# The recurrent stage of a two-block network: TensorE's order written by hand as bursts between groups of eight large matmuls

## The chip, the core and the metric

The kernel runs on one core of a Trainium2 chip. The metric is device time in microseconds (us) of one launch. A core has five engines with instruction queues of their own: TensorE (PE; its weight loads are shown apart as PEld), VectorE (DVE), ScalarE (ACT), GpSimd (POOL) and SyncE (SP). Each runs its instructions in the order of its queue. DMA transfers are issued from one of these queues and wait there for what they depend on.

## What is computed

Two transformer blocks on 512 tokens of width 1024, all in fp32. The first block (two layers of attention with a feed-forward part) is not touched by the change. The second is cut here to what matters:

```python
h = rms_norm_2(x, pre_mix_norm)
p_r, p_k, p_v, p_c, z_rwkv, z_conv = split(h @ w_in)       # 1024 each, p_c 2048
y_rwkv = rwkv7_time_mix(h, p_r, p_k, p_v, ...)             # 16 heads of 64; S is 64x64 for each head
  # step t:  S = S*w_t + (S a_t) b_t + v_t k_t ;  y_t = S r_t ; group norm; + bonus; * g ; @ w_rwkv_out
y_conv = conformer_conv(p_c, ...)                          # u*sigmoid(gate), causal conv of 31 taps over the
                                                           # tokens, layer norm, silu, @ w_conv_out
merged = sigmoid(z_rwkv) * y_rwkv + sigmoid(z_conv) * y_conv
x = x + rms_norm_2(merged @ w_out, post_mix_norm)
x = x + rms_norm_2(ffn(rms_norm_2(x)), post_ffn_norm)
```

The first line to the last but one are the stage that this text calls the recurrent stage.

## The kernel before

**Large products.** A 1024x1024 weight is taken in blocks of 1024x128. `wload` loads a block (SP's queue) into one of two `raw` buffers; ScalarE rounds it to the high half `wh` (L160), VectorE subtracts to get the low half `wl` (L161). A product of such a block with the 512 tokens (`hT_h`, `hT_l`: the halves of h) is 24 matmuls of 128x512: high by high (L274), high by low (L275) and low by high (L277), summed in one PSUM bank. `h`, `l` and `raw` have two buffers each.

**The recurrence in chunks.** The 512 tokens are eight chunks of 64; heads go in pairs j = 0..7 and pairs in groups of two, g = 0..3. `pair_in(j)` makes r, k, v and the gates of a pair from large products. `pair_out(j)` makes decays (L979 to L987), bonus (L1006), the 64x128 Gram matmuls (L1024) and transposes to token order (L1040). `solve(g)` inverts the unit triangular 64x64 matrices of a group: their 16x16 diagonal blocks by forward substitution on VectorE, in 15 steps of a product (L1093) and a reduction (L1095), each as two instructions for the two halves of the partitions. The blocks go through DRAM into that layout and back (L1076, L1085, L1097, L1100, on GpSimd's queue). Then two sets of 64 small 32x32 matmuls (L1107, L1113; below: quads) and an identity product ahead of the first (L1104) join 16x16 blocks to 32x32 ones, VectorE transposes (L1102, L1118), and further small matmuls (L1143 among them) join the rest. `chain(g)` runs over the chunks in order: four small matmuls (L1160, L1169), a copy of half the result by ScalarE (L1171) and half by VectorE (L1172), four more (L1176), an addition on VectorE (L1179, with `ds` made by GpSimd, L1165), four outputs (L1182). A chunk needs the one ahead of it. `post(g)` normalises and gates the outputs (L888 ff.).

**The conv branch.** `conv_in(f)` makes c = u * sigmoid(gate) for 128 channels and stores it in DRAM; `conv(f)` loads it into a tile `c` (one buffer, SP's queue) and runs 30 VectorE instructions over 128x512 (L1228, the taps). The sum over channels, mean, and layer norm follow after the last.

**The end of the stage.** 16 gates z (`gate`), `mapped` by w_rwkv_out into `cm`, layer norm, `mapped` by w_conv_out, the sum `m` split into `mer_h`, `mer_l`, and the product with w_out (`rows_proj`, `ready` holding half of its weights).

**What sets the order.** The code calls these functions in an order given by the strings `ORD` and the counts `FI` (conv_in and gates) and `CV` (conv). Every engine's order then comes from a scheduler which goes by readiness and by the offsets `O` that `high_priority` gives to each function. On TensorE it puts small matmuls singly between large ones wherever they become ready. All the stage's DMAs but the weights and a few loads are issued from GpSimd's queue (`DQ`).

Of the kernel before, what the change touches and what calls it, by code (L numbers as in the profile page):

```python
# [72 lines left out]
def _constants():  # L73
    oh, mask = _t5_onehot()
    i = np.arange(P)
    same = i[:, None] // 64 == i[None, :] // 64
    blk = np.concatenate([same, i[:, None] % 32 < 16, i[:, None] % 32 == np.arange(32),
                          (i[:, None] == i[None, :]) - same / 64], 1).astype(np.float32)
    tri = (i[:, None] % 64 < np.arange(65)[None, :]).astype(np.float32)
    return {"c_t5_oh": oh, "c_t5_mask": mask, "c_nb_mask": _nb_masks(), "c_blk": blk, "c_tri": tri}  # L80
# [7 lines left out]
def tile_two_blocks(ctx: ExitStack, tc: tile.TileContext, A, out):  # L88
# [36 lines left out]
    W["n"] = 0  # L125

# [24 lines left out]
    def wload(src, a, b, views=None, into=None):  # L151
# [454 lines left out]
    with ExitStack() as es:  # L606
# [206 lines left out]
        blk = pm.tile([P, 2 * P + 33], F32, name="blk")  # L813
# [49 lines left out]
    with ExitStack() as es:  # L863
        es.enter_context(lows)
# [4 lines left out]
        nc.vector.memset(smask[:, ::C], 0.0)  # L869
        two = blk[:, :P:64]  # L870
        i32 = blk[:, P + 1 : P + 33]
        centre = blk[:, P + 33 :]
        BANKS.update(ps=[0, 1, 2], po=[3, 4, 5], ca=[6], cb=[7], cc=[6, 7])

        def col_rstd(sq, rhs, eps, op, expand, role="po", scale=1.0):

            ps = pst(role)
# [3 lines left out]
            r = cs.tile([P, 8], F32, tag="r8" + role, name="r8")  # L881
# [4 lines left out]
            ps = pst(role)  # L886
# [7 lines left out]
        with ExitStack() as es2:  # L894
            el = es2.enter_context(tc.tile_pool(name="el", bufs=1))

            SH = 1

            def et(tag, n=T, bufs=1):
                return el.tile([P, n], F32, tag=tag, name=tag, bufs=bufs)  # L900

            def shifted(src, scale=None, **kw):

                sh = el.tile([P, T + 2], F32, tag="sh", name="sh", bufs=SH)
                nc.gpsimd.memset(sh[:, 0:1], 0.0)
                nc.scalar.activation(sh[:, 1 : T + 1], src, AF.Copy, **({} if scale is None else {"scale": scale}))
                return sh[:, 0:T]

            def group_tiles(g):
                q = g % 2  # L910
                G = Ctx()
                X_ = big_tile(f"X{q}", [P, 2, NC_, 2, P])
                G.X = lambda i: X_[:, i]
                G.SV, G.BKT = (big_tile(f"{n}{q}", [P, 2, NC_, 2, C]) for n in ("SV", "BKT"))
                ra = big_tile(f"RA{q}", [P, 2, 2, NC_, C])
                G.RB, G.AB = ra[:, 0], ra[:, 1]
                G.D2 = cs.tile([P, 2, NC_], F32, tag=f"D2{q}", name="D2", bufs=1)
                return G

            def chunks(t):  # L920
                return t.rearrange("p (c t) -> p c t", t=C)

            def pair_in(j):

                fs = slice(j * P, (j + 1) * P)

                def one(v):
                    return V_[v][:, j : j + 1]

                rkv = et("rkv", 3 * T + 2 * C, 2)  # L930
                nc.gpsimd.memset(rkv[:, 0:C], 0.0)
                nc.gpsimd.memset(rkv[:, C + 3 * T :], 0.0)
                for i in range(3):
                    dst_ = rkv[:, C + i * T : C + (i + 1) * T]
                    hl = ahead.pop(0) if ahead else wload(wcols(w_in, 0, KD, i * D + j * P, P), KD, P)
                    o = proj_units([hl])[0]
                    sh = shifted(o, scale=one(("mu_r", "mu_k", "mu_v")[i]))
# [475 lines left out]
```

## Time and profile before

| | us |
|---|---|
| median of 3 runs | 2462.03 (2459.45 to 2467.74) |
| profiled execution, own time | 2471.44 |
| its span, first to last instruction | 2469.7 |
| of it: ahead of the recurrent stage (0 to 1272.5) | 1272.5 |
| the recurrent stage (1272.5 to 2047.7) | 775.2 |
| behind it (product with w_out, feed-forward part) | 422.0 |

All numbers of the trace come from the profiled execution. TensorE is busy 96% of the span and VectorE 51%; a mean granted TensorE clock of 0.972 belongs to it. In the rows below, times are us from the start of the span; "busy" of a matmul can overlap the next one's, since they are pipelined, so the distance of two starts tells what one costs.

### The profile page before, as it was taken

To read this page: it belongs to the slowest core of one execution; us is meant where nothing else is said; L and a number is where in the kernel's file an instruction comes from. 1 tells how busy PE (TensorE), PEld (TensorE's weight loads), DVE (VectorE), ACT (ScalarE), POOL (GpSimd) and SP (SyncE) were. 2 spreads that over 40 slices of the span, in tenths; PEclk is the share of its full clock that TensorE was granted. 3 is DMA by queue.
4 is the path that set the end of the run, shared out by engine and by line. 5 is a ranking of instruction groups with operands and counts; after the bars stand their busy time and mean duration, and the time that the engine had idled before them with its cause. 6 is when DMAs were issued, how large, how long until landed. Compare 5 with 4: busy or idle time off the path is not lost. (4 is left out here: it accounts for less than half of the span.)

```text
span 2469.7 us, 34315 instructions
## 1 busy us (share of the span) xinstructions
PE 2377.3 (96%) x13667; PEld 1869.2 (76%) x13667; DVE 1250.3 (51%) x2083; ACT 934.9 (38%) x1681; POOL 287.2 (12%) x455
## 2 busy tenths in 40 slices
PE   7899999999999999999999899999989999999998
PEld 6756888888887788888886676666667777888887
DVE  4376532143434642223446877588587764422232
ACT  4365432142344542222346344444344343422231
POOL 1000120000100000000012223233142101000000
PEclk9999999999999999999999999899799999999999
DMA  7320763143542263332232222123125454533321
GB/s 202 107 77 35 217 185 98 55 134 106 154 120 79 65 184 96 94 102 93 70 91 82 76 90 71 60 72 92 54 80 174 124 171 148 162 96 95 100 95 60
DMA packets 294240, 263.39 MB, mean 107 GB/s; under 512 B 13904, under 2 KB 260756, under 8 KB 293696
## 3 DMA queue, kind: packets, MB, share of 16 engines
q1 hardware_dynamic: 274648, 208.82, 28.3%
q0 software_dynamic: 10352, 30.02, 3.8%
q10 hardware_dynamic: 9080, 22.37, 3.0%
q8 instruction: 107, 1.75, 0.3%
q14 instruction: 53, 0.43, 0.1%
HBM read 226.33 MB, written 34.83 MB: 106 GB/s over the span
## 5 line engine op out<-in xcount | busy, mean ns | idle before, releaser
L274 PE MATMUL p<-hT_h,wh 128*128 128x512 f32 (+1 forms) x1776 | 686.7, 391 | 7.0 <-DVE cc L1218 3.3
L275 PE MATMUL p<-hT_l,wh 128*128 128x512 f32 (+1 forms) x1776 | 685.7, 390 | 0.0
L161 DVE TENSOR_TENSOR wl<-raw,wh 128x1024 fp32r<-128x1024 f32 (+2 forms) x348 | 410.8, 1184 | 424.5 <-ACT wh L160 360.2
L160 ACT ACTIVATE wh<-raw 128x1024 fp32r<-128x1024 f32 (+2 forms) x348 | 352.2, 1015 | 633.9 <-PE p L275 418.9
L277 PE MATMUL p<-hT_h,wl 128*128 128x512 f32 (+1 forms) x1776 | 449.1, 388 | 7.7 <-DVE wl L161 7.7
L274 PEld LDWEIGHTS p<-hT_h,wh 128*128 128x128 f32 x1776 | 340.3, 192 | 75.4 <-DVE cc L1218 4.5
L275 PEld LDWEIGHTS p<-hT_l,wh 128*128 128x128 f32 x1776 | 340.2, 192 | 66.1 <-issue 2.5
L277 PEld LDWEIGHTS p<-hT_h,wl 128*128 128x128 f32 x1776 | 322.4, 190 | 73.2 <-DVE wl L161 8.1
L168 PE MATMUL p<-wh,fh 128*128 128x512 f32 x528 | 206.1, 390 | 1.5 <-ACT memv L376 0.8
L169 PE MATMUL p<-wl,fh 128*128 128x512 f32 x528 | 205.9, 390 | 0.0
L170 PE MATMUL p<-wh,fl 128*128 128x512 f32 x528 | 205.2, 389 | 0.0
L1228 DVE SCALAR_TENSOR_TENSOR acc<-c,dwc,acc 128x512 f32<-128x512 f32 x240 | 186.0, 775 | 4.5
L300 DVE TENSOR_TENSOR fT<-sg,p 128x384 f32<-128x384 f32 (+1 forms) x88 | 46.8, 552 | 258.7 <-PE p L277 249.5
L192 POOL TENSOR_SCALAR rstd<-ss 128x1 f32<-128x1 f32 x24 | 9.2, 383 | 1445.6 <-ACT junk L188 1445.5
L175 DVE TENSOR_TENSOR fl<-fT,fh 128x512 fp32r<-128x512 f32 x66 | 45.1, 691 | 144.4 <-ACT fh L174 144.4
L168 PEld LDWEIGHTS p<-wh,fh 128*128 128x128 f32 x528 | 99.1, 188 | 23.0 <-ACT memv L376 1.2
L169 PEld LDWEIGHTS p<-wl,fh 128*128 128x128 f32 x528 | 99.1, 188 | 20.3
L170 PEld LDWEIGHTS p<-wh,fl 128*128 128x128 f32 x528 | 99.1, 188 | 20.3
L174 ACT ACTIVATE fh<-fT 128x512 fp32r<-128x512 f32 x66 | 40.8, 628 | 182.7 <-PE p L169 174.8
L168 PE MATMUL p<-wh,hT_h 128*128 128x256 f32 (+1 forms) x256 | 91.7, 359 | 2.6 <-ACT v L536 2.0
L169 PE MATMUL p<-wl,hT_h 128*128 128x256 f32 (+1 forms) x256 | 90.2, 353 | 0.6 <-DVE wl L161 0.6
L170 PE MATMUL p<-wh,hT_l 128*128 128x256 f32 (+1 forms) x256 | 89.0, 351 | 0.0
(328 smaller groups left out, 3053.5 us busy)
## 6 DMA issues: line engine op xcount, KB each, us to landing
raw<-in_w_gu SPq DMA_DIRECT2D x88, 512.0 KB
raw<-in_w_in SPq DMA_DIRECT2D x56, 512.0 KB
raw<-in_w_down SPq DMA_DIRECT2D x44, 512.0 KB
raw<-in_ffn_w_gate SPq DMA_DIRECT2D x22, 512.0 KB
raw<-in_ffn_w_up SPq DMA_DIRECT2D x22, 512.0 KB
raw<-in_ffn_w_down SPq DMA_DIRECT2D x22, 512.0 KB
raw<-in_w_in_b SPq DMA_DIRECT2D x20, 512.0 KB
xs<-xt POOLq DMA_DIRECT2D x19, 512.0 KB, 4.0
```

The costliest lines, as they stand in the source:

```text
L160: nc.scalar.activation(to(h), fr(raw), AF.Copy)
L161: nc.vector.tensor_tensor(to(l), fr(raw), to(h).bitcast(F32), ALU.subtract)
L168: nc.tensor.matmul(ps, lhsT=lh, rhs=rh, start=start, stop=False)
L169: nc.tensor.matmul(ps, lhsT=lh, rhs=rl, start=False, stop=False)
L170: nc.tensor.matmul(ps, lhsT=ll, rhs=rh, start=False, stop=stop)
L174: nc.scalar.activation(h, src, AF.Copy)
L175: nc.vector.tensor_tensor(l, src, h.bitcast(F32), ALU.subtract)
L274: nc.tensor.matmul(o[:, c], lhsT=h[:, k, :], rhs=hT_h[:, k, c], start=k == 0, stop=False)
L275: nc.tensor.matmul(o[:, c], lhsT=h[:, k, :], rhs=hT_l[:, k, c], start=False, stop=False)
L277: nc.tensor.matmul(o[:, c], lhsT=l[:, k, :], rhs=hT_h[:, k, c], start=False, stop=k == KD - 1)
L300: nc.vector.tensor_tensor(dst(fT[:, f, :]), src(sg), src(ps[1]), ALU.mult)
L1228: nc.vector.scalar_tensor_tensor(acc, c[:, t : t + T], dwc[:, t, f : f + 1], acc, ALU.mult, ALU.add)
```

## The change

TensorE's order in the recurrent stage is no longer the scheduler's but that of the code (`manual_schedule` for PE alone; the other engines are scheduled as before). `drive()` walks through a list of units (a unit is one product of 24 large matmuls), and every unit yields after each eight. At a yield, the five streams `chains, outs, solves, posts, ends` are asked in turn; each issues a burst of its small matmuls if its own due time has come, by a count of time in which a group of eight takes `QUANTUM` = 1.85 and a burst the first number of its own yield; the second number is how long the stream then rests. A unit's weights are issued one unit ahead. The list is: pairs and conv_ins mixed, 16 gates, eight maps by w_conv_out, eight by w_rwkv_out. Small parts change along with it:

- The subtraction for `wl` goes in turn to VectorE and to GpSimd.
- `solve` substitutes in 8x8 blocks: 7 steps of two VectorE instructions on all partitions. Six quads instead of two (256 small matmuls more in each solve) and a second identity product join them; `at` and `ttd` are moved by four DMAs each instead of two; the transposes of L1118 go, and three PSUM copies that VectorE makes (L1213 in the new code, L1222 twice) come in, besides ScalarE's.
- The three gate weights of a pair come in one tile; `col_rstd` is two bursts (`sums`, `per_token`); `post` loads its two inputs into the group's free `X` tiles; the taps are paced one at a time; `cc` has two buffers.
- The conv branch is mapped first; the merged result goes into `hT_h`, `hT_l`. Layer norm sits in the stream `ends` and begins while the last chain runs.

```diff
+    W["sub"] = [nc.vector]
-            nc.vector.tensor_tensor(to(l), fr(raw), to(h).bitcast(F32), ALU.subtract)
+            W["sub"][W["n"] % len(W["sub"])].tensor_tensor(to(l), fr(raw), to(h).bitcast(F32), ALU.subtract)
...
+        W["sub"] = [nc.vector, nc.gpsimd]
...
+        def dense(hl, xh=..., xl=..., cut=KD):
+            (h, l), ps = hl, pst()
...
+                        n += 2 - part
+                        if n % 8 == 0 and n < 3 * KD:
+                            yield
+            return ps
...
-                for t in range(1, 16):
-                    p3 = pr[:, : t * t].rearrange("p (j s) -> p j s", s=t)
-                    for q in parts:
-                        nc.vector.tensor_tensor(p3[q], tt[q, :t, :t], at[q, None, :t, t].to_broadcast([q.stop - q.start, t, t]), ALU.mult)
-                    for q in parts:
-                        nc.vector.tensor_reduce(tt[q, :t, t], p3[q], AX.X, ALU.add)
+            for t in range(1, 8):
+                p4 = pr[:, : 2 * t * t].rearrange("p (m j s) -> p m j s", m=2, s=t)
+                nc.vector.tensor_tensor(p4, tt[:, :, :t, :t], at[:, :, None, :t, t].to_broadcast([P, 2, t, t]), ALU.mult)
+                nc.vector.tensor_reduce(tt[:, :, :t, t], p4, AX.X, ALU.add)
...
+            nc.vector.transpose(dt, dd)
+            yield 0, SOLVE_LAT
+            de = s2("de")
+            nc.scalar.activation(de, quad(of(e), of(dt), True), AF.Copy)
+            yield 1.3, 2.5
+            pa, pb = quad(of(de), of(dd)), quad(of(dd), of(de))
+            dd, dt = s2("dd"), s2("dt")
+            nc.vector.tensor_copy(dt, pb)
+            nc.scalar.activation(dd, pa, AF.Copy)
+            yield 1.2, 2.5
+            de = s2("de")
+            nc.scalar.activation(de, quad(lambda i: diag[i], of(dt), True), AF.Copy)
+            yield 1.3, 2.5
+            pb, pa = quad(of(dd), of(de)), quad(of(de), of(dd))
...
+                for t in range(1, 31):
+                    nc.vector.scalar_tensor_tensor(acc, c[:, t : t + T], dwc[:, t, f : f + 1], acc, ALU.mult, ALU.add)
+                    yield None, TAP
...
+        CCB, SOLVE_LAT, CHAIN_LAT, TAP = 2, 25.0, 1.8, 1.3
+        QUANTUM, GAP = 1.85, 1
...
+            hl, since, idle = units[0][0](), 0, 0.0
+            for i, (_, run, pre) in enumerate(units):
+                while pre is not None and not pre():
+                    now += 0.5
+                    idle += 0.5
+                    burst()
+                nxt = units[i + 1][0]() if i + 1 < len(units) else None
+                for _ in run(hl):
+                    now += QUANTUM
+                    since += 1
+                    if since >= GAP:
+                        since = 0
+                        burst()
+                hl = nxt
...
+        with tc.manual_schedule(engines={mybir.EngineType.PE}):
+            drive()
```

The names in the rows below are tiles with a running number; `p` is a PSUM bank. TensorE's queue before, in group 0's chain while a pair's product runs (L1176 is a state update, L1182 an output):

```order
L1176 MATMUL p_12447<-SV_11129,BKT_11130 64x64
L274 MATMUL p_13160<-hT_h,wh 128x512
L1176 MATMUL p_12447<-SV_11129,BKT_11130 64x64
L275 MATMUL p_13160<-hT_l,wh 128x512
L1176 MATMUL p_12447<-SV_11129,BKT_11130 64x64
L274 MATMUL p_13160<-hT_h,wh 128x512
L1176 MATMUL p_12447<-SV_11129,BKT_11130 64x64
```

In the order after, a chain's bursts stand as follows (L1278 reads the state, L1282 and L1301 make outputs, L1163 and L1166 are the identity product and a quad of group 1's solve, L934 and L935 large):

```order
L1278 MATMUL p_12104<-SV_9831,X_9830 64x64 x4
L1282 MATMUL p_12105<-X_9830,SV_9831 64x64 x4
L1163 MATMUL p_12120<-blk,ident 128x512
L1166 MATMUL p_12120<-dt,e 32x32 x64
L934 MATMUL p_12095<-hT_h,wh 128x512
L935 MATMUL p_12095<-hT_l,wh 128x512
L934 MATMUL p_12095<-hT_h,wh 128x512
L935 MATMUL p_12095<-hT_l,wh 128x512
L934 MATMUL p_12095<-hT_h,wh 128x512
L935 MATMUL p_12095<-hT_l,wh 128x512
L934 MATMUL p_12095<-hT_h,wh 128x512
L935 MATMUL p_12095<-hT_l,wh 128x512
```

Where single small matmuls stood between single large ones, whole bursts now stand between groups of eight; the burst behind this group (L1295, the state update into p_12104) reads what VectorE copies out of L1278's result.

VectorE's queue before, at a copy of the chain (L1172; L1228 are taps, L1218 ends a conv_in, L1011 and L997 belong to a pair_out):

```order
L1228 SCALAR_TENSOR_TENSOR acc<-c,dwc,acc 128x512 x2
L1218 TENSOR_TENSOR cc<-p_11851,cc 128x512
L1172 COPY SV_9831<-p_11074 64x2x64
L1228 SCALAR_TENSOR_TENSOR acc<-c,dwc,acc 128x512
L1011 TENSOR_TENSOR X_12581<-rkv,le 128x8x64
L1228 SCALAR_TENSOR_TENSOR acc<-c,dwc,acc 128x512 x2
L997 TENSOR_TENSOR ls<-ls,rkv 128x512
```

VectorE's queue after, at the place of the bursts above (L1347 are taps, L1290 the chain's copy, L1298 its addition, L1205 and L1213 belong to the solve):

```order
L1347 SCALAR_TENSOR_TENSOR acc<-c,dwc,acc 128x512 x4
L1290 COPY SV_9831<-p_12104 64x2x64
L1347 SCALAR_TENSOR_TENSOR acc<-c,dwc,acc 128x512 x2
L1205 STREAM_TRANSPOSE dt<-dd 128x512
L1347 SCALAR_TENSOR_TENSOR acc<-c,dwc,acc 128x512 x8
L1298 TENSOR_TENSOR SV_9831<-p_12104,ds 64x2x64 x2
```

Ten taps and a transpose stand between the copy and the addition of one chunk.

GpSimd's queue after, in a solve (L1201 and L1204 move the substituted blocks out and back):

```order
L893 TENSOR_TENSOR r_10663<-r_10663,neg_half 128x8
L1201 DMA ttd_9683<-tt 64x8x8 x4
L163 TENSOR_TENSOR wl<-raw,wh 128x1024
L1204 DMA dd<-ttd_9683 32x16x32 x4
L1107 DMA bvd_9635<-so 128x512
```

Before, the same two DMA steps (L1097, L1100) had one store between them; now a weight's subtraction stands there.

## Rows read from the trace of the kernel before

**Rows 1.** Stretch: us, busy (instructions) of PE, PEld, DVE, ACT, POOL, clock, DMA share, GB/s.

```profile
1272.50:2047.70 775.20, 733.99 (x5543) 528.41 (x5542) 566.30 (x1001) 346.25 (x628) 198.69 (x281) 0.94 0.32 95
```

**Rows 2.** TensorE's waits in the recurrent stage: total us, times, longest.

```profile
PE p L277 <- DVE wl L161: 7.7, 1, 7.7
PE p L888 <- ACT ysq L884: 5.8, 5, 2.2
...
```

**Rows 3.** Timeline of TensorE, large matmuls alone: start, us of one.

```profile
1299.77 0.40 PE L274 MATMUL p<-hT_h,wh 128*128 128x512 f32 x1
...
1300.24 0.40 PE L274 MATMUL p<-hT_h,wh 128*128 128x512 f32 x1
```

**Rows 4.** The same view where Gram matmuls stand between large ones.

```profile
1305.95 2.57 PE L1024 MATMUL p<-X,bk 64*128 64x128 f32 x24 [0.28 <-PE p L277]
...
1309.35 0.48 PE L1024 MATMUL p<-X,bk 64*128 64x128 f32 x2
...
1310.20 0.48 PE L1024 MATMUL p<-X,bk 64*128 64x128 f32 x2
```

**Rows 5.** The same view, state updates and transposes between large matmuls.

```profile
1430.94 0.45 PE L1176 MATMUL p<-SV,BKT 128*64 128x64 f32 x8
...
1483.76 0.33 PE L1176 MATMUL p<-SV,BKT 128*64 128x64 f32 x2
...
1484.45 0.33 PE L1176 MATMUL p<-SV,BKT 128*64 128x64 f32 x2
...
1487.07 0.50 PE L277 MATMUL p<-hT_h,wl 128*128 128x512 f32 x1
1487.41 0.60 PE L1040 MATMUL p<-ident,rkv 128*128 128x128 f32 x4
```

**Rows 6.** Costliest lines of the stage: busy, mean ns, idle before.

```profile
L1228 DVE SCALAR_TENSOR_TENSOR acc<-c,dwc,acc 128x512 f32<-128x512 f32 x240 | 186.0, 775 | 4.5
L1093 DVE TENSOR_TENSOR pr<-tt,at 64x1 f32<-64x1 f32 (+14 forms) x120 | 38.5, 321 | 3.4
L1095 DVE TENSOR_REDUCE tt<-pr 64x1 f32<-64x1 f32 (+14 forms) x120 | 28.2, 235 | 3.6
L1118 DVE STREAM_TRANSPOSE RA<-dT 32x512 f32<-32x512 f32 x16 | 11.2, 701 | 0.4
L1113 PE MATMUL p<-dd,de 32*32 32x32 f32 x512 | 5.7, 193 | 1.9 <-issue 1.9
L1104 PE MATMUL p<-blk,ident 128*128 128x512 f32 x8 | 5.3, 747 | 0.0
```

**Rows 7.** Timeline of VectorE and GpSimd: a subtraction alone, and one beside GpSimd.

```profile
1334.99 1.23 DVE L161 TENSOR_TENSOR wl<-raw,wh 128x1024 fp32r<-128x1024 f32 x1 [0.84 <-PE p L277]
1343.79 3.36 DVE L161 TENSOR_TENSOR wl<-raw,wh 128x1024 fp32r<-128x1024 f32 x1
1344.01 2.05 POOL L1056 TENSOR_TENSOR rkv<-bk,D 128x512 f32<-128x512 f32 x2
```

**Rows 8.** Timeline of GpSimd and VectorE: the first solve's DMAs, first product and transpose.

```profile
1350.41 1.37 POOL L1076 DMA_DIRECT2D abd<-RA  x2 [1.59 <-ACT RA L1031]
1363.85 0.14 DVE L1093 TENSOR_TENSOR pr<-tt,at 64x1 f32<-64x1 f32 x1
1391.11 1.76 POOL L1097 DMA_DIRECT2D ttd<-tt  x2 [10.79 <-DVE tt L1095]
1397.89 2.59 POOL L1100 DMA_DIRECT2D dd<-ttd  x4 [3.89 <-DMA ttd<-tt]
1405.56 0.70 DVE L1102 STREAM_TRANSPOSE dt<-dd 128x512 f32<-128x512 f32 x1
```

**Rows 9.** Three stretches inside the stage, columns as in rows 1.

```profile
1530.00:1630.00 100.00, 95.91 (x900) 69.05 (x899) 73.66 (x120) 50.17 (x89) 31.25 (x39) 0.85 0.25 73
1745.00:1800.00 55.00, 53.51 (x219) 33.39 (x220) 27.11 (x47) 21.17 (x44) 10.75 (x12) 0.72 0.16 49
1870.00:1945.00 75.00, 75.00 (x702) 52.65 (x700) 60.74 (x96) 28.09 (x54) 17.25 (x25) 1.00 0.46 141
```

More of the change, by code (lines that the diff above doesn't have):

```diff
@@ L1150, in chain @@
[L1150 to L1157 removed]
+                        nc.tensor.matmul(ps[q32(i), q32(c)], lhsT=lhsT(i)[:, c, :], rhs=rhs(i)[:, c, :],
+                                         start=not eye, stop=c == 15 or not eye, tile_position=(32 * i, 32 * i))
@@ new lines, in solve @@
+            yield 1.2, 2.5
+            ps = pst("po")
+            for c in range(16):
+                for i in (1, 3):
+                    nc.tensor.matmul(ps[q32(i), q32(c)], lhsT=dT[q32(i), c, :], rhs=rr[q32(i), c, :],
+                                     start=True, stop=True, tile_position=(32 * i, 32 * i))
+            for i in (1, 3):
+                nc.scalar.activation(ABf[q32(i), :, 0:32], ps[q32(i)].rearrange("p (q t) -> p q t", t=32), AF.Copy)
+            yield 1.2, 2.5
+            while outs_done < 2 * g + 2:
+                yield 0, 0.5
@@ L1223, in conv @@
+        def conv():
+            for f in range(KD):
+                while f >= len(convs):
+                    yield 0, 1.0
+                c = cs.tile([P, 30 + T], F32, tag="c", name="c", bufs=1)
                 nc.sync.dma_start(c, cd[f])
@@ new lines, in tile_two_blocks, with outs @@
+        nil = el.tile([64, 1024], F32, tag="bk", name="nil")
+        nc.gpsimd.memset(nil, 0.0)
+        for t in ttd:
+            DQ[10].dma_start(t.rearrange("p a b -> p (a b)"), nil)
+        def outs():
+            nonlocal outs_done
+            for j in range(KD):
+                while not hasattr(pairs.get(j), "done") or (j % 2 == 0 and posts_done < j // 2 - 1):
+                    yield 0, 0.5
+                if j % 2 == 0:
+                    groups[j // 2] = group_tiles(j // 2)
+                yield from pair_out(j, groups[j // 2])
+                outs_done += 1
@@ new lines, in solves, with enter_ln @@
+        def solves():
+            nonlocal solves_done
+            for g in range(4):
+                while not hasattr(pairs.get(2 * g + 1), "grams"):
+                    yield 0, 0.5
+                yield from solve(g, groups[g])
+                solves_done += 1
+            enter_ln()
+        def enter_ln():
+            es2.close()
+            nonlocal lnp
+            lnp = es4.enter_context(tc.tile_pool(name="ln", bufs=1))
+            L.ct_h, L.ct_l = (cat(t[:, :4], t[:, 4:]) for t in (lnp.tile([P, KD, T], F32R, name=n) for n in ("ct_h", "ct_l")))
@@ new lines, in ends, with drive, burst @@
+        def ends():
+            nonlocal ln_done
+            yield from conv()
+            while lnp is None or posts_done < 3:
+                yield 0, 0.5
+            yield from layer_norm()
+            ln_done = True
+        lnp, es4 = None, ExitStack()
+        def drive():
+            now = 0.0
+            streams = [[s, 0.0] for s in (chains(), outs(), solves(), posts(), ends())]
+            def burst():
+                nonlocal now
+                for s in list(streams):
+                    while s[1] <= now:
+                        got = next(s[0], None)
+                        if got is None:
+                            streams.remove(s)
+                            break
+                        now += got[0] or 0.0
+                        s[1] = (s[1] if got[0] is None else now) + got[1]
+                        if got[0]:
+                            break
+            hl, since, idle = units[0][0](), 0, 0.0
[12 more added lines that the diff above has]
+                hl = nxt
+            while streams:
+                now += 0.5
+                burst()
+            return now, idle
```

799 lines of the change are left out of this document (416 added, 383 removed).

## The prediction

> **What bounds the kernel now.** I read the table of stretches first. The recurrent stage is 775.2 us, and TensorE is busy 734.0 of them, VectorE 566.3, ScalarE 346.3, GpSimd 198.7 [rows 1]. So TensorE sets the end, and it stands idle for only 775.2 − 734.0 = 41.2 us. The list of its waits shows that these are scattered: one of 7.7 us for a subtracted low half, five of 5.8 together for ScalarE's square in the group norm, and many smaller ones [rows 2]. Whatever the change gives must come out of how the 734 are spent, and three views take them apart.
>
> First the timeline of large matmuls alone: two of them start 0.47 us apart from the next two, 0.235 each [rows 3]. 1728 large ones in the stage cost some 400 us at that pace. Second, the timeline where small ones stand singly between them. A Gram part in a run of 24 costs 2.57/24 = 0.107 us, yet a large matmul with one small one (two parts) costs 1310.20 − 1309.35 = 0.85, which is 0.85 − 0.235 − 0.214 = 0.40 more than its members [rows 4]. For a state update (8 parts in 0.45, so 0.056 each) it is 1484.45 − 1483.76 = 0.69, so 0.69 − 0.235 − 0.112 = 0.34 more; in front of transposes a large one takes 1487.41 − 1487.07 = 0.34, only 0.11 over 0.235 [rows 5]. Each change from large to small and back therefore costs 0.1 to 0.4 us. Third, the granted clock: 0.94 over the stage [rows 1], that is 775 × 0.06 = 46 us lost against the upper level, 2.4 GHz, in stretches at the lower one, 1.2 GHz. It is 0.85 where much small work is mixed in and 0.72 in the last solve and chain, and 1.00 where large products fill TensorE without a gap [rows 9].
>
> **The change part by part.** Outside the stage nothing changes. Work is summed at the upper clock level, lost clock apart.
>
> A. Changes between large and small. In the order of instructions there are 296 places before where a large matmul is followed by a small one, and 113 after: 183 fewer. Bounds by the rows above are 183 × 0.11 = 20 and 183 × 0.40 = 73 us. Most of the removed ones are of the chain's and the Gram's kind (0.34 to 0.40), some are transposes; I take 0.30: **−55**.
>
> B. Quads. Four more for each solve, in four solves, are 1024 small matmuls, 2048 parts of the trace. A set of 512 parts now takes 5.7 us, 0.0111 each [rows 6]: +22.8. The four additional identity products cost 5.3/4 = 1.3 each [rows 6]: +5.3. They stand on TensorE, the bound, and nothing hides them: **+28**. They could be at most cheaper by their share of changes already counted in A.
>
> C. Waits. Before, TensorE could take whatever was ready; now it stops at the next burst until its input is there, and all large matmuls behind it stop too. So VectorE's and GpSimd's queues, still ordered by the scheduler, must deliver within a group of eight (8 × 0.235 = 1.9 us) and the bursts beside it. The place shown in the change: between the chain's copy and its addition VectorE has ten taps and a transpose, 10 × 0.775 + 0.70 = 8.5 us [rows 6, 8]; TensorE meanwhile has the rest of the burst, an identity product, a quad and eight large matmuls, some 5.5 us. Excess 3.0. The same comparison over all 64 half-steps of the four chains gives 33 us, of which half lies in the last chain, where layer norm's subtractions and splits stand between copy and addition (10.2 against 3.9 and 12.5 against 3.7), and 12.6 in the first. With what slack the chain has at five such places I take 27. The solves: the path from the first DMA to the transpose is 1350.4 to 1406.3, 56 us, of which 1363.9 to 1391.1, 27 us, were substitution with taps between its instructions [rows 8]; 14 instructions instead of 60 take this to 27 × 14/60 = 6, the path to 35, and with 4 us of doubt for the order of taps and DMAs to 31 to 39. TensorE has about 33 us of work there: 2 us each, 8 in all. Weights: 10, as the first and the like of rows 2 are now, since SP's queue still holds them behind the load of `c` that waits for the last tap. GpSimd's hold on VectorE (next paragraph): 10. Together 55 instead of 41: **+14**. If the bursts' inputs are all early it is −41; the other end is rival 2.
>
> D. The subtractions. 36 of the stage's 79 go to GpSimd. VectorE gives up 36 × 1.23 = 44 us. But the rows show what that does: a subtraction that takes 1.23 us alone took 3.36 with GpSimd's 2.05 us of products over as many bytes beside it [rows 7], so VectorE stood still about as long as GpSimd worked. 34 or so by 2.05 is 70 us in which an instruction of VectorE with two operands in SBUF can be held. A hold meets a given one of the chain's 128 links with 70/740 and lasts 1 us on average: 12, taken as 10 in C. The subtraction also stands between the solve's two DMA steps on GpSimd's queue (2.05 us, in the 31 to 39 above) and ahead of the chain's `ds`. The Trainium skill, page "SBUF — State Buffer", section "SBUF: two separate sides", says that VectorE with two SBUF inputs and GpSimd take an exclusive lock on one port pair for a whole instruction; the trace agrees with 3.36 against 1.23 us, and by that rule the move gains nothing.
>
> E. VectorE's total. Substitution: 240 instructions, 38.5 + 28.2 = 66.7 us [rows 6], become 56 of about the same length, 16: −51. The transposes of L1118 go, −11 [rows 6]; the subtractions −44; new copies out of PSUM +7, by the 0.70 of a 128x512 transpose. 566 − 99 = 467, plus 70 of holds, 537 of some 740: still not the bound as a total, so it costs only in C. Cover for all this is TensorE's work; where it is gone is C.
>
> F. Clock. The removed singles are what stands in the stretches at 0.72 and 0.85, and behind the last chain 384 large matmuls now run without a stop, as the stretch at 1.00 does [rows 9]. All 46 back is one end; in proportion to the waits (55 for 41) it is 46 × 55/41 − 46 = +16. I take the middle: **−15**.
>
> Sum: −55 + 28 + 14 − 15 = **−28 us**. On the profiled execution's 2471.4 that is 2443; on the median of 2462.0, 9 us below it, **2434**.
>
> **The rivals.**
>
> 1. The streams meet their dates. Waits stay at 41 or so and the clock comes back whole: −55 + 28 + 0 − 46 = −73, **2389**. For it: the taps are paced, and VectorE has a third of its time free. Against it: the order of VectorE was not fixed, and ten taps stand inside one half-step.
>
> 2. VectorE sets the pace of the chains, slower than before. Each of the 64 half-steps finds one tap (0.775) ahead of its copy or addition: 50 us; the excess of whole runs of taps and splits comes on top without slack, 33; the solves' path takes the upper end, 6 each, 24. Waits 107 instead of 41, +66: −55 + 28 + 66 − 15 = +24, **2486**. It decides from waits of 41 + 42 = 83 us on, where the sum is nothing. For it: a stopped TensorE has no other work, by its fixed order; and GpSimd's subtractions hold VectorE [rows 7]. By the page named above, the holds alone would bring this about, since 70 us of GpSimd's work stand against 44 saved. Against it: the new streams leave a group of eight, 1.9 us, between a link and its use, more than two taps.
>
> 3. Changes between large and small are cheap, and the reordering is worth nothing much: 183 × 0.11 = 20. −20 + 28 + 14 − 15 = +7, **2469**, about no change. For it: 0.11 in front of transposes; most changes may be like that. Against it: the two distances of 0.85 and 0.69.
>
> **How the numbers follow.** A measurement of this kernel can tell some 0.3% from no change: 2454.6 to 2469.4 is "same". My own case (2400 to 2454) 0.42; rival 1, below 2400, 0.20; rival 3 and other sums that come out near nothing 0.12; rival 2, above 2469, 0.26. So faster 0.62, same 0.12, slower 0.26. The likeliest is 2434. For the range I take as one end rival 1 with the changes at their upper price (−73 + 28 − 46 = −91 gives 2371; I stop at 2378) and as the other rival 2 with the clock as it is now (−55 + 28 + 66 = +39 gives 2501; I stop at 2495): **2378 to 2495**, leaving out about 1 in 10 on either side.
>
> **What the profile after would show.** A: rows of a small form between single large ones are gone; large matmuls lie 0.235 apart in eights, and a burst with its change costs its parts and 0.3. B: quads total some 34 us (11.4 + 22.8) where they are now 11.4. C: TensorE's waits in the stage at 55 and not 41, most behind the chain's copies and additions, in the last and the first chain; if they are behind `ds` or `wl`, it is GpSimd. D: subtractions on VectorE and taps of 2 to 3 us where GpSimd subtracts, and GpSimd's own at 2 us or more. F: the clock of the stage at 0.96 or more, and 1.00 over the last 90 us of maps. I am wrong if the waits come to over 83 us, if the taps stretch by more than 70 us in all, or if a change costs 0.1.

## The result and the profile after

The changed kernel takes 2486.7 us (span of the profiled execution 2483.7; median of 6 runs, 2479.7 to 2492.7) against 2467.3 of the kernel before on the same chips: a ratio of 1.008, 95% interval 1.0054 to 1.0106. It is slower by 19 us. The forecast was 2434, faster; the time is that of the second rival, 2486.

The stretches of the changed kernel, columns as in [rows 1]:

```profile
0.00:1272.50 1272.50, 1232.29 (x6245) 998.09 (x6245) 538.72 (x927) 471.93 (x894) 71.94 (x149) 0.99 0.39 114
1272.50:2062.00 789.50, 679.65 (x7598) 536.25 (x7599) 492.09 (x767) 370.92 (x672) 294.04 (x343) 0.90 0.31 92
2062.00:2483.70 421.70, 410.19 (x1881) 341.36 (x1880) 144.98 (x156) 118.41 (x162) 16.57 (x32) 0.99 0.35 108
```

Outside the recurrent stage nothing moved. The stage is 789.5 us where it was 775.2 [rows 1], 14.3 more. TensorE is busy 679.7 us, 54.3 less than before; but it waits 789.5 − 679.7 = 109.8 us where it waited 41.2, 68.6 more. The granted clock fell from 0.94 to 0.90. So the order did make the work shorter, and all of that and more went into waits. Who TensorE waits for in the stage (total, times, longest):

```profile
PE p L1295 <- DVE SV L1290: 25.1, 10, 9.2
PE p L1166 <- DVE dt L1205: 24.8, 3, 14.5
PE p L170 <- DVE rkv L962: 19.8, 5, 7.5
PE p L1166 <- issue: 18.7, 9, 2.5
PE p L1278 <- DVE SV L1298: 11.9, 4, 9.4
```

Against [rows 2], where the longest of all was 7.7, these are few, long and nearly all behind VectorE: the chain's copy (L1290) and addition (L1298), the solve's transpose (L1205), and a read of a PSUM bank (L962). The fourth, 18.7 us in quads (L1166), waits for nothing that this list can name.

Three of them can be read from the timelines. First the bank. The large products have three PSUM banks; a pair's gate weights need three at once, right behind the product of v. Its bank comes free when VectorE has run L962. TensorE, VectorE and GpSimd at that place:

```profile
1352.18 0.40 PE L172 MATMUL p<-lo,lowl 64*128 64x512 f32 x2
1359.90 0.80 PE L170 MATMUL p<-lo,lowh 128*128 128x512 f32 x1 [7.32 <-DVE rkv L962]
```

```profile
1353.45 5.73 DVE L1347 SCALAR_TENSOR_TENSOR acc<-c,dwc,acc 128x512 f32<-128x512 f32 x3
1359.11 0.74 DVE L962 SCALAR_TENSOR_TENSOR rkv<-p,der,rkv 128x512 f32<-128x512 f32 x1
```

```profile
1353.26 2.48 POOL L163 TENSOR_TENSOR wl<-raw,wh 128x1024 fp32r<-128x1024 f32 x1
1355.70 2.94 POOL L1109 TENSOR_TENSOR rkv<-bk,D 128x512 f32<-128x512 f32 x2
```

Three taps, 2.3 us by the 0.775 of [rows 6], take 5.73 while GpSimd subtracts and multiplies beside them. That is 3.4 of the 7.32 us; the rest of the wait is the order of VectorE's queue.

Second the solve of group 2. GpSimd's queue, then VectorE's, then TensorE's:

```profile
1668.76 0.76 POOL L1178 DMA_DIRECT2D abd<-RA  x1 [1.75 <-ACT RA L1131]
...
1704.69 1.36 POOL L1201 DMA_DIRECT2D ttd<-tt  x2 [0.32 <-issue]
...
1707.87 2.34 POOL L163 TENSOR_TENSOR wl<-raw,wh 128x1024 fp32r<-128x1024 f32 x1
1710.15 2.64 POOL L1204 DMA_DIRECT2D dd<-ttd  x4
```

```profile
1686.54 0.16 DVE L1198 TENSOR_TENSOR pr<-tt,at 128x2 f32<-128x2 f32 x1
...
1702.34 0.25 DVE L1199 TENSOR_REDUCE tt<-pr 128x14 f32<-128x98 f32 x1
...
1709.37 9.43 DVE L1347 SCALAR_TENSOR_TENSOR acc<-c,dwc,acc 128x512 f32<-128x512 f32 x8 [2.67 <-ACT acc L1343]
1718.71 0.70 DVE L1205 STREAM_TRANSPOSE dt<-dd 128x512 f32<-128x512 f32 x1
```

```profile
1719.47 1.34 PE L1166 MATMUL p<-dt,e 32*32 32x32 f32 x84 [14.50 <-DVE dt L1205]
```

The 14 instructions of the substitution, which the prediction put at 6 us, run from 1686.5 to 1702.6, 16 us, with taps and other work between them. The last block lands in DRAM at 1707.5 (issued at 1705.4, landing 2.1 us later), but the way back is issued only behind a subtraction, at 1710.15, 2.6 us later. The last block is back at 1715.3 (1712.1 and 3.2); then the eight taps, stretched to 9.43 us, hold the transpose until 1718.7, another 3.4. TensorE, which may not go round its next burst, stops for 14.5 us. Without the subtraction and the taps it would still have stopped for some 8.5 us, by an estimate from these rows: the path itself, 1668.8 to 1719.4, is 51 us long.

Third the supply. In the second of two quads that stand back to back, TensorE runs dry in the middle:

```profile
1747.09 0.61 PE L1166 MATMUL p<-dd,de 32*32 32x32 f32 x49
1750.16 0.87 PE L1166 MATMUL p<-dd,de 32*32 32x32 f32 x79 [2.46 <-issue]
```

The list of waits has no cause for this, but the DMA queues of 1747.5 to 1750.2 have a transfer of instructions:

```profile
q8 instruction: 1, 0.02, 2.5%
```

Each of the eight stops of some 2 us or more in quads has one such transfer that begins less than 0.7 us from its start, and the stage has 60 of them in 789.5 us. So TensorE probably waits there for its own instructions; the rows show that the two come together, and no run here separates them.

### The profile page after: what moved, and what is told of

Same layout as the page of the kernel before. It is cut to its first block, busy times and chain, and to the rows that moved or that the text cites. A ratio compares the mean times of both kernels' runs of the same rounds, so it can differ in the third digit from the quotient of the medians.

```text
span 2483.7 us, 38312 instructions
## 1 busy us (share of the span) xinstructions
PE 2322.1 (93%) x15723; PEld 1875.7 (76%) x15723; DVE 1175.8 (47%) x1850; ACT 961.3 (39%) x1727; POOL 382.5 (15%) x524
## 5 line engine op out<-in xcount | busy, mean ns | idle before, releaser
L162 ACT ACTIVATE wh<-raw 128x1024 fp32r<-128x1024 f32 (+1 forms) x340 | 349.9, 1032 | 659.1 <-PE p L277 363.8
L163 DVE TENSOR_TENSOR wl<-raw,wh 128x1024 fp32r<-128x1024 f32 (+1 forms) x305 | 361.4, 1188 | 432.4 <-ACT wh L162 351.3
L276 PE MATMUL p<-hT_h,wh 128*128 128x512 f32 (+1 forms) x1328 | 492.0, 376 | 3.6 <-ACT wh L162 2.1
L277 PE MATMUL p<-hT_l,wh 128*128 128x512 f32 (+1 forms) x1328 | 492.1, 376 | 0.0
L279 PE MATMUL p<-hT_h,wl 128*128 128x512 f32 (+1 forms) x1328 | 308.3, 374 | 0.0
L276 PEld LDWEIGHTS p<-hT_h,wh 128*128 128x128 f32 x1328 | 251.1, 189 | 49.7 <-ACT wh L162 2.6
L277 PEld LDWEIGHTS p<-hT_l,wh 128*128 128x128 f32 x1328 | 251.3, 189 | 45.0 <-issue 0.6
L1347 DVE SCALAR_TENSOR_TENSOR acc<-c,dwc,acc 128x512 f32<-128x512 f32 x240 | 207.5, 865 | 20.4 <-ACT acc L1343 15.7
L934 PE MATMUL p<-hT_h,wh 128*128 128x512 f32 x448 | 200.2, 447 | 0.7 <-ACT hn L846 0.7
L935 PE MATMUL p<-hT_l,wh 128*128 128x512 f32 x448 | 188.8, 421 | 0.0
L932 PE MATMUL p<-hT_h,wl 128*128 128x512 f32 x448 | 120.3, 411 | 0.0
```

The lines of the kernel that those rows point to most:

```text
L163: W["sub"][W["n"] % len(W["sub"])].tensor_tensor(to(l), fr(raw), to(h).bitcast(F32), ALU.subtract)
L276: nc.tensor.matmul(o[:, c], lhsT=h[:, k, :], rhs=hT_h[:, k, c], start=k == 0, stop=False)
L277: nc.tensor.matmul(o[:, c], lhsT=h[:, k, :], rhs=hT_l[:, k, c], start=False, stop=False)
L279: nc.tensor.matmul(o[:, c], lhsT=l[:, k, :], rhs=hT_h[:, k, c], start=False, stop=k == KD - 1)
L932: nc.tensor.matmul(ps, lhsT=l[:, k, :], rhs=xh(k), start=False, stop=k == KD - 1)
L934: nc.tensor.matmul(ps, lhsT=h[:, k, :], rhs=xh(k), start=k == 0, stop=False)
```

## The experiments

Each time is a median; "changed" is the changed kernel (2487), and ratios are to the kernel before, run on the same chip.

**Subtractions back on VectorE.**

```diff
-        W["sub"] = [nc.vector, nc.gpsimd]
+        W["sub"] = [nc.vector]
```

> The changed kernel with all subtractions for the low halves on VectorE again (none on GpSimd). In the profile of the changed kernel TensorE waits 110 us in the stage, 82 of them for VectorE. Theory 1 (GpSimd's subtractions hold VectorE and stand in the queue of the solve's DMAs): the taps' mean of 865 ns falls to about 780, TensorE's waits fall by 20 to 35 us, time 2455 to 2470. Theory 2 (the order of VectorE's queue that the scheduler makes is what is late, the holds matter little): VectorE has 43 us more to do in the same order, waits stay within 10 us of 110 or grow, time 2480 to 2500.

Measured: 2448.2, ratio 0.9925 (0.9897 to 0.9953). One line takes away 38 us, and the rest of the change is then faster than the kernel before. Its stage:

```profile
1272.50:2027.80 755.30, 671.08 (x7640) 531.20 (x7639) 503.89 (x806) 366.43 (x670) 206.11 (x306) 0.93 0.33 96
```

Waits fall from 110 to 84, and busy time by 8.6 with the same order on TensorE, as the clock rises from 0.90 to 0.93. Theory 1 holds, with a time below its range. Of the 26 us of waits that go, 11 were behind the chain's copy, 9 at the solves and 5 at the bank, where there are left:

```profile
PE p L1166 <- DVE dt L1205: 16.2, 3, 6.2
PE p L170 <- DVE rkv L962: 15.0, 5, 6.4
PE p L1295 <- DVE SV L1290: 13.8, 8, 9.1
```

**The same subtractions in the kernel before.** One edit to the kernel before: every second subtraction of the stage on GpSimd.

> The kernel before, with one edit: in the recurrent stage every second subtraction for the low halves goes to GpSimd. In the streamed kernel the same edit turned out to cost 38 us (2448 without it, 2487 with it). Theory 1 (GpSimd's work of about 2.4 us each holds VectorE and delays the weights and the solves whatever TensorE's order is): the kernel before gets slower by 15 us or more. Theory 2 (it costs so much only because TensorE's order is fixed and cannot go round a late input): within 8 us of 2466.

Measured: 2520.5, ratio 1.0194 (1.0151 to 1.0237), 50 us slower. It is not TensorE's fixed order that makes them dear; TensorE's waits rise from 41 to 71 there too, and its busy time by 20, and the taps grow to 820 ns. The scheduler placed all engines' instructions anew for this edit, so another order can be a part of the 50:

```profile
1272.50:2097.00 824.50, 753.73 (x5575) 542.44 (x5574) 573.04 (x960) 344.66 (x628) 284.85 (x323) 0.92 0.30 89
```

**Which way they cost.** Subtractions on VectorE, and useless work on GpSimd beside every second large weight, first with read operands, then without (one loop or the other; the comments name the run):

```diff
+        if W.get("pad") and W["n"] & 1 and (a, b) == (KD, P):
+            nc.gpsimd.tensor_copy(W["pt"][:, :1], h[:, 0, :1].bitcast(F32))
+            for _ in range(4):
+                nc.gpsimd.tensor_tensor(W["pt"], W["pt"], W["blk"][:, :256], ALU.subtract)   # pad_tt
+            for _ in range(7):
+                nc.gpsimd.memset(W["pt"], 0.0)                                               # pad_ms
```

> The streamed kernel with all subtractions on VectorE (2448), and for every second large weight some 2.4 us of useless work on GpSimd once its high half is there: four subtractions over 128x256 that read and write tiles nobody waits for. Theory 1 (GpSimd's instructions with two operands in SBUF hold VectorE's): taps grow from 775 to 850 ns or more, and most of the 38 us comes back: 2470 to 2490. Theory 2 (the cost was that the weights' halves come late and that GpSimd's queue delays the solves' DMAs and the chain's ds): the weights are as early as without it, 2445 to 2465, taps under 800 ns.

> The same as pad_tt, but the useless work is seven memsets over 128x256, which read nothing and take GpSimd about as long. Theory 1 (it is the two read operands that hold VectorE): taps stay at 775 to 790 ns, and what is left is the queue's delay, 2450 to 2460, clearly under pad_tt. Theory 2 (it is GpSimd's queue): the same time as pad_tt, within 6 us.

Measured: 2468.5 with read operands (ratio 1.0007, 0.9983 to 1.0032), 2448.5 without (0.9921, 0.9893 to 0.9948). The taps, in the changed kernel, with the subtractions back, in pad_tt and in pad_ms (count, busy us, mean ns):

```profile
L1347 DVE SCALAR_TENSOR_TENSOR acc<-c,dwc,acc 128x512 f32<-128x512 f32 x240 | 207.5, 865 | 20.4 <-ACT acc L1343 15.7
```

```profile
L1347 DVE SCALAR_TENSOR_TENSOR acc<-c,dwc,acc 128x512 f32<-128x512 f32 x240 | 186.0, 775 | 16.7 <-ACT acc L1343 12.2
```

```profile
L1354 DVE SCALAR_TENSOR_TENSOR acc<-c,dwc,acc 128x512 f32<-128x512 f32 x240 | 196.5, 819 | 17.3 <-ACT acc L1350 12.7
L167 POOL TENSOR_TENSOR pad<-pad,blk 128x256 f32<-128x256 f32 x140 | 136.6, 976 | 10.3
```

```profile
L1354 DVE SCALAR_TENSOR_TENSOR acc<-c,dwc,acc 128x512 f32<-128x512 f32 x240 | 187.9, 783 | 15.1 <-ACT acc L1350 10.5
L167 POOL MEMSET pad<- 128x256 f32 x245 | 76.7, 313 | 12.7
```

Their stages:

```profile
1272.50:2050.00 777.50, 671.65 (x7625) 530.34 (x7624) 532.86 (x805) 364.95 (x669) 350.92 (x482) 0.92 0.32 93
```

```profile
1272.50:2025.90 753.40, 666.47 (x7598) 527.19 (x7599) 506.40 (x804) 364.68 (x668) 290.93 (x587) 0.92 0.33 96
```

77 us of memsets in GpSimd's queue cost nothing; 137 us of subtractions that nobody waits for cost 20, between the two theories of `pad_tt`. The memsets took less time than was expected of them, but the length does not explain it: all of VectorE's work grew by 532.9 − 503.9 = 29 us beside the 137 us of reads, 0.21 for each, and by 2.5 beside the 77 us of memsets, 0.03 for each. So about half of the 38 us is GpSimd holding VectorE. What the other 18 are is open. They are not more holding: with 35 of the 71 subtractions of 1.24 us moved away VectorE would have 503.9 − 43.4 = 460.5 us, and it had 492.1 in the changed kernel, 32 more, hardly over 29. Nor do they show as low halves that TensorE waits for: of the 12 us between the profiled executions of the changed kernel and `pad_tt`, waits are 4 (110 for 106) and TensorE's busy time is 8, at a clock of 0.90 for 0.92.

**The bank.**

```diff
-                psg = pst()
+                psg = pst("po")
```

> The changed kernel with the third product of a pair's gate weights put into a bank of the small matmuls' set (three banks) and not into the set of the large ones. In the changed kernel this product waits 19.8 us in all (five times, 7.5 the longest) for VectorE's shift of v, which has to read the bank out first. Theory 1 (a stopped TensorE has nothing else to do, so each of its waits counts in full): these waits go, time falls by 15 to 20 us to about 2468. Theory 2 (the streams only wait at the next place instead, because the chain of VectorE's work sets the pace): the wait reappears behind the chain's copies and additions or the solves, time within 6 us of 2487.

Measured: 2491.8, ratio 1.0092 (1.0062 to 1.0122): no gain. The 19.8 us went, and came up elsewhere:

```profile
PE p L1166 <- DVE dt L1205: 40.4, 4, 14.6
PE p L1295 <- DVE SV L1290: 27.5, 12, 9.2
```

TensorE came to the solve's quad earlier and waited there 15.6 us more. Theory 2.

**A longer rest ahead of the first quad.**

```diff
-        CCB, SOLVE_LAT, CHAIN_LAT, TAP = 2, 25.0, 1.8, 1.3
+        CCB, SOLVE_LAT, CHAIN_LAT, TAP = 2, 40.0, 1.8, 1.3
```

> The changed kernel with the rest that a solve takes before its first quad raised from 25 to 40 us (about eight groups of eight large matmuls more). In the changed kernel that quad waits 24.8 us in all (14.5 the longest) for the transpose behind the substitution. Theory 1 (bursts are placed earlier than their input can be there): this wait falls under 6 us, time falls by 12 to 20 us, to about 2470. Theory 2 (the time is only pushed on, since the chains that follow start later and the last one ends later): time within 6 us of 2487, with waits of the chains or at the maps in its place.

Measured: 2463.2, ratio 0.9988 (0.9961 to 1.0014), 24 us less than the changed kernel. No wait for the transpose is left in the list; waits are 97 and the clock 0.92. Theory 1, with a little more than its 12 to 20 us: the burst was placed before its input could be there.

**Layer norm tile by tile.** A yield behind each of its eight tiles.

```diff
+                yield (None if f else 0.6), 3.0
-            yield 0.6, 14.0
+            yield 0, 4.0
...
+                yield (None if f else 0.7), 4.0
-            yield 0.7, 8.0
+            yield 0, 4.0
```

> The changed kernel with the layer norm of the conv branch issued one tile of 128 channels at a time between the last chain's bursts, not all eight in two blocks. In the changed kernel the last chain waits once 9.4 and once 9.2 us behind VectorE's subtractions, products and splits of the layer norm. Theory 1 (VectorE's queue holds whole blocks ahead of the chain's copy): these two waits fall under 4 us together, time falls by 10 to 16 us. Theory 2 (VectorE's order follows readiness and not the order in the code, so it bunches them anyway): the waits stay, time within 6 us of 2487.

Measured: 2477.7, ratio 1.0046 (1.0018 to 1.0074), 9 us less. The wait behind the addition fell from 11.9 to 2.5, the longest behind the copy from 9.2 to 3.8. Theory 1, a little smaller than expected.

**Without the taps.** Subtractions on VectorE, 29 of 30 taps left out (so the kernel no longer computes the conv; two runs).

```diff
-                for t in range(1, 31):
+                for t in range(1, 2):
```

> The streamed kernel with all subtractions on VectorE, and 29 of the 30 taps of the conv left out (232 instructions of 0.775 us, 180 us of VectorE's 504). TensorE waits 84 us in its stage with them. Theory 1 (the taps that the scheduler puts ahead of the streams' links are what TensorE waits for): waits fall to 45 us or less, what is left being the supply of quads (16.5), the layer norm in the last chain (18) and little else; time 2400 to 2415. Theory 2 (it is the length of the dependent paths through DMA, ScalarE and PSUM that is late): waits stay above 65, time above 2425.

Measured: 2429.5, ratio 0.9835 (0.9773 to 0.9896): 19 us less than with them, waits 72 for 84. Theory 1 said 45, and it is theory 2 whose figures hold (over 65 and over 2425). With VectorE busy 340 us and not 504, the chain still waits:

```profile
PE p L1166 <- issue: 21.9, 10, 3.2
PE p L1295 <- DVE SV L1290: 20.5, 6, 9.1
PE p L1278 <- DVE SV L1298: 12.5, 4, 8.6
```

So taps in VectorE's queue are a smaller part than the prediction's rival made them; of these 33 us in the chain some 18 are layer norm (9.1 and 8.6).

**Large matmuls between two quads.** Subtractions on VectorE, and a yield between `pa` and `pb`, and in the same way between the second such two, during which streams that use the same banks rest.

```diff
-            pa, pb = quad(of(de), of(dd)), quad(of(dd), of(de))
+            pa = quad(of(de), of(dd))
+            hold[0] = True
+            yield 0.7, 0.0
+            hold[0] = False
+            pb = quad(of(dd), of(de))
...
```

> The streamed kernel with all subtractions on VectorE, and a group of eight large matmuls between the two quads that before stood back to back (other streams that use the same banks rest there, except the chain). In it TensorE waits 16.5 us in quads for nothing that the profile shows, eight times for 2 to 2.7 us, each in the second of two quads. Theory 1 (TensorE uses such small matmuls up faster than its instructions come, and eight large ones give the supply time): these waits fall under 4 us, time falls by 8 to 12 us to about 2438. Theory 2 (it is a fixed cost of each quad or of reading the first one's copy): they stay, time within 6 us of 2448.

Measured: 2436.4, ratio 0.9857 (0.9812 to 0.9901), 12 us less than 2448. The waits by "issue" in quads fell from 16.5 to 1.8, as theory 1 has it:

```profile
PE p L1168 <- issue: 1.8, 6, 0.5
```

**Together.** Subtractions on VectorE, rest 40, layer norm spread; then the split quads besides; then the bank besides.

> The streamed kernel with three edits at once: all subtractions on VectorE, 40 us of rest ahead of a solve's first quad, layer norm issued tile by tile. Alone they gave 2448, 2463 and 2478 instead of 2487, that is 38, 24 and 9 us. Theory 1 (each takes away waits of its own, and a wait of TensorE counts in full): the solves' 16 and the layer norm's 17 us left in the first of them go, 2415 to 2430. Theory 2 (they take away the same lateness of VectorE): 2440 to 2450.

> The streamed kernel with four edits at once: all subtractions on VectorE, 40 us of rest ahead of a solve's first quad, layer norm tile by tile, and a group of large matmuls between two quads. The first three together gave 2430, with 16.6 us left of waits in quads for nothing that the profile shows. Theory 1 (waits of different kinds add up): these go as they did alone, 12 us, to 2415 to 2422. Theory 2 (solves get longer by four groups, and the last chain then ends too late for the maps): 2428 or more.

> The kernel with the four edits, and besides the third product of a pair's gate weights in a bank of the small matmuls' set. Alone in the changed kernel this edit gave nothing (2492 for 2487): 19.8 us of waits for the bank went, and 15.6 more came up at the solves' transposes. Theory 1 (it moved there because the solve's path was the longest one; with 40 us of rest the solve has slack, so the gain now stays): 8 to 13 us less than the four edits. Theory 2 (VectorE's order sets the pace anyway): within 5 us of the four edits.

Measured: 2429.9 (ratio 0.9837, 0.9800 to 0.9874), 2428.0 (0.9837, 0.9798 to 0.9877) and 2425.2 (0.9842, 0.9795 to 0.9889). The first three give 57 of the 71 us that they gave one by one; the stage is 42 us shorter than before:

```profile
1272.50:2005.20 732.70, 668.38 (x7613) 529.25 (x7612) 508.20 (x804) 369.50 (x671) 204.11 (x306) 0.94 0.34 99
```

The other two do nothing more that can be measured, though the split was worth 12 alone: its 16.6 us of waits did go (2.3 left), but small ones came up at many places (60.0 for 64.3 in all), and TensorE's busy time rose by 4.4. In the last one the bank's wait only moved from the gate weights to the next large product, which now needs that bank (11.2 us there for 14.3). Theory 1 was missed in both of these runs. These three kernels beat both kernels of the case by some 40 and 60 us.

**Finer and coarser bursts.** Subtractions on VectorE, bursts after every four or every sixteen large matmuls; then four with the rest of 40 and the layer norm.

```diff
-                        if n % 8 == 0 and n < 3 * KD:
+                        if n % 4 == 0 and n < 3 * KD:
-        QUANTUM, GAP = 1.85, 1
+        QUANTUM, GAP = 0.925, 1      # fine4, best_fine4
+        QUANTUM, GAP = 1.85, 2       # gap2, with n % 8 as before
```

> The streamed kernel with all subtractions on VectorE (2448), bursts allowed after every four large matmuls instead of eight: 139 places where a large matmul is followed by a small one instead of 108. Theory 1 (a change costs 0.3 us, as in the prediction): work at the upper clock grows by 31 x 0.3 = 9 us, and waits do not fall since a group of four is only 0.9 us: 2455 to 2465. Theory 2 (small matmuls in the chain cost the rest, not the changes): work within 3 us, time 2442 to 2452.

> The streamed kernel with all subtractions on VectorE (2448), bursts only after every sixteen large matmuls: 70 places where a large matmul is followed by a small one instead of 108. Theory 1 (each burst then has twice the time for its input): waits fall from 84 to 50 or less and changes by 38 x 0.3 = 11 us, 2405 to 2425. Theory 2 (the chains last longer, and the last one ends behind the gates, so TensorE waits for its end): 2450 or more, with long waits ahead of the maps.

> The streamed kernel with all subtractions on VectorE, 40 us of rest ahead of a solve's first quad, layer norm tile by tile (together 2430), and bursts allowed after every four large matmuls (2442 for 2448 alone, with the chain's waits down from 26 to 16 us and the solves' up from 16 to 26). Theory 1 (the chain's waits fall as they did alone, and the solves now have slack): 2415 to 2425. Theory 2 (31 more changes at 0.3 us take it back): 2428 to 2440.

Measured: 2442.0 (ratio 0.9899, 0.9861 to 0.9938), 2460.4 (0.9980, 0.9955 to 1.0005) and 2434.9 (0.9861, 0.9811 to 0.9912). With 31 more changes TensorE's busy time did not rise (663 for 671 us), with 38 fewer it did not fall (670). Coarser bursts did not shorten the waits either (93 for 84); finer ones moved them from the chain (26 to 16) to the solves (16 to 26). In best_fine4 the chain's waits were not shorter than with eights. Where theory 1 of `fine4` had 9 us more of work, there were 8 less, which speaks against 0.3 us for a change; but the clock differs too (0.94 for 0.93). The time of `gap2` is that of its theory 2, without the long waits ahead of the maps (2.6 us there). So none of these gives the price of a change.

## Why the prediction was wrong

The sum was −55 + 28 + 14 − 15. Measured by the same terms it was a busy time 54.3 us shorter and waits 68.6 us longer.

- **C, waits, is the step that failed: +14 charged, +68.6 measured.** Its reason, that TensorE before "could take whatever was ready", is not right as it stands: both kernels run TensorE's queue in its order, and only who placed the instructions differs. The prediction summed VectorE's excess over the chains' half-steps (27), which came out at 25.1 + 11.9 = 37, and it named the right places: the two in the last chain that it gave 10.2 and 12.5 us of VectorE's work waited 9.4 and 9.2. It gave the solves 8 where they took 24.8, for the path from the first DMA to the transpose, which it put at 31 to 39 us, was 51 in group 2 (1668.8 to 1719.4), most of it by the substitution's 16 us for 6; the rest of 25 written into the order was too short. The weights, charged 10, waited 2.4. And it missed two kinds altogether: 19.8 us for a bank, which only stood in the count of `ps` banks against the three products of a pair's gate weights, and 18.7 us of quads back to back, where instructions were probably still on their way. Of the second kind [rows 6] had the sign, 1.9 us of idle time by "issue" ahead of L1113; what it would become with three times the quads was not asked.
- **D, the subtractions, were charged 10 us and are worth 38.** The rows were there: 3.36 us beside GpSimd for 1.23 alone [rows 7]. The prediction took the hold's chance at each of the chain's links; but whatever is late on VectorE is passed on to TensorE through the solves and the banks as well (9 and 5 us of the 26 that go with the edit). About half of the 38 is holding, by the runs with useless work; the rest is open. The Trainium skill's rule (page "SBUF — State Buffer", section "SBUF: two separate sides"), that only a GpSimd instruction that reads SBUF locks out a VectorE instruction with two operands there, agrees with the two runs with useless work: 819 ns a tap beside reads, 783 beside memsets, for 775. The prediction set it down as a reason of rival 2; into its sum it let 10 us.
- **F, the clock, had the wrong sign.** It was to give back 15 us; it fell from 0.94 to 0.90. In the changed kernel and its variants it goes roughly with the waits: 0.94 with 64 us (three edits), 0.93 with 84, 0.92 with 97, 0.91 with 103, 0.90 with 110; not strictly, since the run with the bank has 0.91 with 121 and the one with coarser bursts 0.91 with 93. Small matmuls have a part of their own: in the kernel before it is 0.72 over 55 us of which TensorE is busy 53.5 [rows 9], and 0.94 over a stage with waits of 41. Nor is it worth what was charged: with the same order on TensorE, busy time differs by 8.6 us between 0.90 and 0.93, where 0.03 of 790 would be 24, since a part of the time at the lower level is waiting anyway. The wait of 14.5 us shows both parts, in the columns of [rows 1]:

```profile
1700.00:1705.00 5.00, 4.97 (x21) 3.10 (x19) 4.24 (x9) 3.03 (x6) 1.80 (x3) 1.00 0.51 125
1712.00:1719.40 7.40, 0.00 (x0) 0.00 (x0) 7.22 (x8) 0.00 (x0) 4.18 (x8) 0.50 0.42 123
1719.40:1722.00 2.60, 2.53 (x130) 2.37 (x131) 2.49 (x5) 0.53 (x1) 0.00 (x0) 0.50 0.02 6
1726.00:1732.00 6.00, 4.71 (x234) 4.03 (x233) 5.90 (x10) 1.44 (x3) 0.00 (x0) 1.00 0.31 90
```

```profile
1722.35 0.63 PE L934 MATMUL p<-hT_h,wh 128*128 128x512 f32 x1
1722.78 0.63 PE L935 MATMUL p<-hT_l,wh 128*128 128x512 f32 x1
```

The clock falls to its lower level while TensorE waits, where that costs nothing, and is still there for the first work behind the wait, where large matmuls start 0.43 us apart and not 0.23.

- **B was right**: quads take 37.4 us busy for 11.4, identity products 11.8 for 5.3 [rows 6], together 32 for the 28 forecast; the stops by "issue" come on top.
- **A was right in its direction and mis-sized**: the busy time fell by 54 in spite of B's 32, so the rest fell by some 86, for 55. By the busy time of the lines 43 of it lie in the chain's four kinds of matmul (102.0 to 59.3), 18 in the transposes to token order (45.5 to 27.2) and 21 in the third eight of the pairs' products, low by high (141.5 to 120.3). How much of this is changes from large to small is open. A burst shows the pieces:

```profile
1790.28 0.39 PE L935 MATMUL p<-hT_l,wh 128*128 128x512 f32 x1
1790.60 0.45 PE L1278 MATMUL p<-SV,X 128*64 128x64 f32 x8
1790.88 0.40 PE L1282 MATMUL p<-X,SV 128*64 128x64 f32 x8
1791.21 2.05 PE L1124 MATMUL p<-X,bk 64*128 64x128 f32 x16
```

The large matmul ahead of it takes 0.32 where 0.23 is its own, and the 16 small parts 0.61, 0.038 each, where 0.056 was charged. The prediction had divided the busy time of eight, 0.45, which overlaps with the next matmul (the same 0.45 stands here); by the distance of starts the change at a state update costs about 0.69 − 0.235 − 2 × 0.038 = 0.38 and not 0.34. So a change was priced a little low by this; the runs with finer and coarser bursts do not settle the rest.

- **E was right**: VectorE is not the bound as a total (492 us busy, 467 forecast and up to 70 of holds). Rival 2's time was right (2486 for 2487, waits 107 for 110), which is partly luck, for its mechanism was right only in part: not a tap ahead of every half-step, as the run without taps shows (12 us of waits), but a few long waits of five different kinds, and GpSimd's subtractions alone are worth more than the whole loss.

## What to carry to other kernels

When an engine's order is fixed by hand, everything behind a late input stops, so list for each burst who makes its input, what stands ahead of that on its queue, and which bank or buffer it needs; a sum of average work does not show a wait of 14 us. Removing one wait is worth something only if the next burst's input is there: the bank gave nothing while the solves were late, and nothing that can be measured once they were not, since its wait moved to the next product. And before moving elementwise work from VectorE to GpSimd, look in the trace for an instruction of VectorE with two operands in SBUF beside one of GpSimd that reads SBUF: here moving some 44 us of work off VectorE made one kernel 38 us slower and the other 50.

## What was not expected of the hardware

- 77 us of GpSimd memsets beside VectorE's taps cost no time (taps 783 ns for 775; all of VectorE's work 2.5 us longer), 137 us of subtractions with read operands cost 20 (819 ns; 29 us longer).
- Two sets of 64 matmuls of 32x32 back to back stop TensorE for 2 to 2.7 us in the second, each time beside one transfer of the queue that brings instructions (0.98 MB in 60 over the changed kernel's stage); eight large matmuls between them take this away (16.5 to 1.8 us).
- The granted clock of the stage fell from 0.94 to 0.90 with TensorE's waits, although the alternation of small and large matmuls that was thought to lower it had gone: in a wait of 14.5 us it fell to 0.50, and 2.6 us of work behind it still ran at 0.50.
